# One-core hybrid transformer: float32r head sums, regrouped inverses and an earlier first preparation in the RWKV layer; a third value tile up front in the neighbourhood attention

## The chip, the core and the metric

The kernel runs on one core of a Trainium2 chip. The metric is the device time of one execution in microseconds (us); the kernel before takes 2552.61 us (median of three runs, 2551.04 to 2557.27). The execution that was profiled took 2547.62 us, with a span from its first to its last instruction of 2545.2 us. The engines are named as the profile names them: PE is TensorE (PEld its weight loads), DVE is VectorE, ACT is ScalarE, POOL is GpSimd, and SP is the queue that issues the DMAs.

## The reference, cut to what matters

Four layers work on 256 latent and 256 context tokens of 1024 features, all in float32. The mixers are grouped-query attention (layers 0 and 3), neighbourhood attention (layer 1) and a bidirectional RWKV-7 (layer 2). Each mixer is followed by a normalization, an MLP with squared ReLU, and another normalization. What the change touches is this:

```
# neighbourhood attention (layer 1)
q, k, v = split(h @ wqkv, 3)
# RWKV (layer 2), per token, 16 heads of 64 features
g  = sigmoid(xg @ g1) @ g2
kk = k * k_k ;  kk = kk * rsqrt(max(sum_head(kk*kk), 1e-12))
# ... two scans over the tokens (forwards and backwards) give y ...
mu = mean_head(y) ; var = mean_head((y - mu)**2)
y  = (y - mu) * rsqrt(var + eps) * lnx_g + lnx_b
bonus = sum_head(r * (k_dir0 + k_dir1) * r_k) * v
y  = ((y + bonus) * g) @ wo
```

## The kernel before

**Products.** Activations lie with features on the partitions and the 512 tokens in the free dimension. A float32 product is made of three float32r products: both operands are split into a high part (a cast to float32r on ACT) and a low part (a subtraction on DVE), and high by high, high by low and low by high are summed in one PSUM bank (`mm3`, L430 to L432; `gemm_v`, L479 to L481, for the values, which have tokens on the partitions). The weights come as 363 tiles of 128x1024, in the order of `plan()`; each is loaded by SP (`load_to`), cast by ACT and completed by DVE (L280), a few tiles ahead of their use (`W.depth`). These tiles, the split activations (`pair`, `k4`) and much else share one ring of 36 SBUF tiles of 128x1024.

**Order.** The program text gives each piece of work its place, and the tile framework's scheduler orders each engine's instructions at build time from that, pulling a piece ahead where its inputs and buffers are free by its own model. On the chip every engine then works strictly in its order.

**Neighbourhood attention, opening.** The layer before ends with its latent tokens last, so `opening` runs the context half of the new layer's first products (tokens 256 to 511, tiles 2 and 3) while the latent half is being normalized: after pass `at[0]` it issues `centre`, after pass `at[1]` it issues `finish` (`finish` is one small sum on PE, L537, two ACT steps, and then the scaling and splitting of the eight feature tiles of `h`). The passes are `values(0)` and `values(1)` for the context tokens; `together` (L848 on) then does the same two value tiles for the latent tokens, feature tile by feature tile as `h` arrives. `values(2)` and `values(3)` follow for all tokens.

**RWKV, up to the recurrence.** Six token-shifted mixtures of `h` are made, each of eight 128x512 tiles: a DVE multiply-add (L1025), an ACT cast and a DVE subtraction (L425). After the receptances, `low` makes three low-rank products in turn: `rw_w1` (decay), `rw_a1` and `rw_g1` (output gate, then a Sigmoid into `sig`), each waiting for its own mixture; the mixture of the keys is made after that of the gate. Then come eight `keys(c)`, and the values in eight steps (four weight tiles by two token halves). The rest is a list `todo` (L1561 on) of pieces with a place on a common axis, sorted: `core(c)` covers c to c+1, `prep(c)` c-2.4 to c-.9, `inverses(c)` c-.65 to c-.1, `post(c)` c+1 to c+1.6, keys -2.6 to -1.5, values -1.35 to .3.

**One c of the RWKV** is one 128-feature tile (two heads).
- `prep(c)`: gate products (`wps`) with Sigmoids on ACT, `unit_k` (square on ACT, head sum `kss` by a matmul with the block matrix `ones64`, two logarithm-table steps), decays (scans), products for both directions, `triangles` (`tps`), `solve`: 16x16 triangular systems on POOL, with DMAs through DRAM before and after (`dr`, `lane`, `rr`, `S`).
- `inverses(c)`: the transpose `R` of `S`, then `corner` (`pa`), `both` (`pb`), `spread`, `level1` (`pv`) and `level1b` (`px`), small 32x32 matmuls that join the solved blocks.
- `core(c)`: eight blocks of 64 tokens in both directions. Each block goes `zps` (PE), copy `z` (ACT), `ups` (PE), copy `u` (ACT), `sps` (PE), one or two DVE steps to the next state `s`, and from there to the next block's `zps`; masked products `nps`, transposes `bkt` and outputs `yps` stand between.
- `post(c)`: `mean` (head sum `gm`), `bonus` (head sum `bo`, transposed values `vT`), `var` (head sum `gv`), `normed`, `gated` (product `g` of `g2` and `sig`), `parts`.

The four head sums of a c are plain float32 matmuls of 128x128 by 128x512. PSUM has eight banks: `ps_mm` has three, `ps_s` two, `ps_x` two, `ps_o` one; the sums, `pa`, `pb`, `vT`, `g` and half of `wps` go through `ps_s`.

Of the kernel before, what the change touches and what calls it, by code (L numbers as in the profile page):

```python
# [36 lines left out]
def plan():  # L37

    g = []
    for i in range(DEPTH):  # L40
        if i % 3 == 0:
            a = i // 3
            g += [("att_wqkv", a, "T", 0, n) for n in (8, 9)]
            g += [("att_wqkv", a, "V", kh, 5) for kh in range(2)]
            g += [("att_wqkv", a, "T", 0, n) for n in range(8)]
            g += [("att_wo", a, "T", 0, n) for n in range(8)]
        elif i % 3 == 1:
            g += [("na_wqkv", 0, "V", kh, 8 + j) for j in range(4) for kh in range(2)]
            for c in range(8):
                g += [("na_wqkv", 0, "T", 0, 8 + c), ("na_wqkv", 0, "T", 0, c)]  # L50
            g += [("na_wo", 0, "T", 0, n) for n in range(8)]
        else:
            g += [("rw_wr", 0, "T", 0, n) for n in range(8)]
            g += [("rw_w1", 0, "L", 0, 0), ("rw_a1", 0, "L", 0, 0), ("rw_g1", 0, "T", 0, 0)]
            g += [("rw_wk", 0, "T", 0, n) for n in range(8)]
            g += [("rw_wv", 0, "V", kh, j) for j in range(4) for kh in range(2)]
            g += [("rw_wo", 0, "T", 0, n) for n in range(8)]
        for w, q in MLP_ORDER:
            if w == "1":
                g += [("mlp_w1", i, "T", 0, 8 * q + n) for n in range(8)]  # L60
            else:
                g += [("mlp_w2", i, "T", q, n) for n in range(8)]
    return g
# [130 lines left out]
def dit_kernel(ctx: ExitStack, tc: tile.TileContext, places, t_in, out, layers=DEPTH):  # L194
# [266 lines left out]
        mm3(ps, w, h[KC - 1], 0, 512, KC - 1, False, True)  # L461
        return ps

    def gemm_v(h, parts, toks):

        out = []
        for x, t in enumerate(toks):
            if x % 2 == 0:
                ps_b = bank(ps_mm, 512, "vps")
# [12 lines left out]
        return out  # L482
# [348 lines left out]
    def natten(i, h, gate, nrm, begun, ends):  # L831
        V = [k4("nV") for _ in range(4)]
        kept = {}

        def values(j, toks):
            def part(kh):
                def go():
                    if (j, kh) not in kept:
                        kept[j, kh] = W.next("na_wqkv", 0, "V", kh, 8 + j)
                    return kept[j, kh]  # L840
                return go

            def go():
                for t, ps in zip(toks, gemm_v(h(), [part(0), part(1)], toks)):
                    act.copy(out=V[t][:, j * 256:(j + 1) * 256], in_=ps)
            return go

        def together():  # L848

            ps = [bank(ps_mm, 512, "vps").rearrange("p (t d) -> p t d", t=2) for _ in range(2)]  # L850
            for c in range(KC):
                for j in range(2):
                    vh, vl = (w[:, (c % 4) * 256:(c % 4) * 256 + 256] for w in kept[j, c // 4])
                    for t in range(2):
                        sh, sl = (h()[c][:, y, t * 128:(t + 1) * 128] for y in range(2))
                        pe.matmul(ps[j][:, t], lhsT=sh, rhs=vh, start=c == 0 and t == 0, stop=False)
                        pe.matmul(ps[j][:, t], lhsT=sh, rhs=vl, start=False, stop=False)
                        pe.matmul(ps[j][:, t], lhsT=sl, rhs=vh, start=False, stop=c == 7 and t == 1)
            for j in range(2):
                for t in range(2):  # L860
                    act.copy(out=V[t][:, j * 256:(j + 1) * 256], in_=ps[j][:, t])

        opening(begun, (0, 1), lambda cnd: [values(0, TOKS[1]), values(1, TOKS[1])] if cnd else [together], at=(0, 0))
        kept.clear()
        values(2, range(4))()
        values(3, range(4))()
        kept.clear()
        h = h()
# [93 lines left out]
    def rwkv(i, hx, gate, nrm, begun, ends):  # L962
# [35 lines left out]
        dve.tensor_scalar(out=ka1, in0=C("k_a", "rw"), scalar1=-1.0, scalar2=1.0, op0=ALU.mult, op1=ALU.add)  # L998


        xx = [pair("xx") for _ in range(4)]


# [102 lines left out]
        made[1](PM)  # L1106
        act.activation(out=lora[:, 0], in_=ps, func=AF.Tanh)
        ps = low("rw_a1", "L", made[1])
        made[2](PM)
        act.copy(out=lora[:, 1], in_=ps)  # L1110
        ps = low("rw_g1", "T", made[2])
        made[3](PM)
        act.activation(out=sig, in_=ps, func=AF.Sigmoid)
        m = made[3](KC)
        W.limit = PLAN.index(("rw_wo", 0, "T", 0, 0))
        W.depth = 2

        def keys(c):
            def go():
                if c == 9:  # L1120
                    W.depth = 1
                keep(c, 1, gemm(W.next("rw_wk", 0, "T", 0, c), m, ALL))
                if c == 7:
                    made[4](PM)
            return go
# [36 lines left out]
        def prep(c):  # L1162
# [5 lines left out]
            def gate_products():  # L1168
# [4 lines left out]
                for x, (key, bias) in enumerate((("sg", "w0"), ("ag", "a0"))):  # L1173
                    for d in range(2):
# [7 lines left out]
                            dve.memset(b8(t)[:, :, 0:1], 0.0)  # L1182
                            dst, ps = b8(t)[:, :, 1:65], b8(ps)
                        todo.append(dict(out=dst, in_=ps, bias=C(bias, "rw")[:, d, c:c + 1]))
                sigmoids(todo)
            out.append(gate_products)

            def unit_k():
                sq = tmp(512, "ksq")
                act.activation(out=sq, in_=k_, func=AF.Square, scale=C("k_k", "rw")[:, c:c + 1])  # L1190
                ps = bank(ps_s, 512, "kss")
# [285 lines left out]
        def post(c):  # L1477
            q = st[c]
            hold = {}

            def mean():
                y = tmp(512, "y")
                act.copy(out=y, in_=q["y"])
                ps = bank(ps_s, 512, "gm")
                pe.matmul(ps, lhsT=ones64, rhs=y, start=True, stop=True)
                dve.scalar_tensor_tensor(out=y, in0=ps, scalar=-1.0 / 64, in1=y, op0=ALU.mult, op1=ALU.add)
                sq = tmp(512, "ysq")
                act.activation(out=sq, in_=y, func=AF.Square)
                hold["y"], hold["sq"] = y, sq

            def bonus():
                ps = bank(ps_s, 512, "bo")
                pe.matmul(ps, lhsT=ones64, rhs=q["rkd"], start=True, stop=True)
                bo = q["rkd"]
                act.copy(out=bo, in_=ps)
# [5 lines left out]
                hold["bo"] = bo  # L1501

            def var():
                ps = bank(ps_s, 512, "gv")
# [8 lines left out]
                affine(y, y, C("lnx_g", "rw")[:, c:c + 1], C("lnx_b", "rw")[:, c:c + 1])  # L1513

            def gated():
                ps = bank(ps_s, 512, "g")
                g2 = sml.tile([128, 128], F32, tag="g2", bufs=1, name="g2")
                sp.dma_start(out=g2, in_=t_in["rws"][c, :, 2])
                pe.matmul(ps, lhsT=g2, rhs=sig, start=True, stop=True)
                y = hold["y"]  # L1520
# [42 lines left out]
        for c in range(8):  # L1563
            main = core(c)
            todo += [(c + x / len(main), f) for x, f in enumerate(main)]
            todo += over(inverses(c), c - .65, c - .1)
            todo += over(post(c), c + 1, c + 1.6) if c < 7 else []
            if c >= RHELD:
                todo.append((c - 2.9, lambda c=c: fetch(c)))
        for c in range(8):  # L1570
# [3 lines left out]
            def step(k, c=c, made_=made_):  # L1574
# [224 lines left out]
```

## Time and profile before

| | us |
|---|---|
| median of three runs (lowest, highest) | 2552.61 (2551.04, 2557.27) |
| the profiled execution | 2547.62 |
| its span | 2545.2 |
| PE busy in the span | 2448.7 (96%) |
| DVE busy | 1664.0 (65%) |
| ACT busy | 1188.7 (47%) |
| POOL busy | 209.2 (8%) |

PE's busy time counts a matmul from its start to its modelled end, and matmuls overlap: a 128x512 float32r matmul lasts 0.39 us and the next starts 0.23 us after it. So what a matmul costs PE is read from start to start, and a full PE still hides nothing else. Lines of a timeline give start, duration, engine, line, operation, output<-inputs and count, and in brackets the idle time before with what ended it.

### The profile page before, as it was taken

The numbers are of one execution on the slowest core, as the hardware profiler recorded it, in microseconds if no ns is written. First come the engines' busy times: TensorE is split into PE (matmuls) and PEld (weight loads), VectorE is DVE, ScalarE is ACT, GpSimd is POOL, SyncE is SP. The second block draws the span as 40 slices with busy tenths as digits, with TensorE's granted clock in tenths as the row PEclk, the third lists the DMA queues.
The fourth block names the chain that finished last, engine by engine and source line by source line (L and its number), as shares of the span: only waits on it lengthen the run. The fifth ranks groups of instructions, "written<-read, shape, count | busy, mean of one in ns | idle before, by whom it ended". The sixth has DMA issues, their size and how long they took to land. (4 is left out here: it accounts for less than half of the span.)

```text
span 2545.2 us, 53184 instructions
## 1 busy us (share of the span) xinstructions
PE 2448.7 (96%) x22337; PEld 2085.8 (82%) x22337; DVE 1664.0 (65%) x3087; ACT 1188.7 (47%) x2226; POOL 209.2 (8%) x383
## 2 busy tenths in 40 slices
PE   8999999999999999999889799899999999998998
PEld 5779888889766988888867677778898888998997
DVE  4567777775566777787786565673567663766555
ACT  3555443244566543334555444544362343465644
POOL 0002000002000110000202112211020000121000
PEclk9999999999999999999999999999999999999999
DMA  8432556642211245665132311210336654223553
GB/s 337 166 127 75 182 189 192 207 157 88 69 55 58 88 152 182 207 205 176 60 112 77 80 28 33 41 20 15 143 107 216 206 184 126 93 68 115 175 184 98
DMA packets 158415, 324.11 MB, mean 127 GB/s; under 512 B 77393, under 2 KB 80993, under 8 KB 158177
## 3 DMA queue, kind: packets, MB, share of 16 engines
q1 hardware_dynamic: 158176, 320.73, 39.8%
q8 instruction: 175, 2.87, 0.5%
q14 instruction: 64, 0.52, 0.1%
HBM read 310.71 MB, written 9.97 MB: 126 GB/s over the span
## 5 line engine op out<-in xcount | busy, mean ns | idle before, releaser
L430 PE MATMUL mm<-h,wh 128*128 128x512 f32 (+1 forms) x1472 | 515.5, 351 | 6.1 <-ACT h L180 4.7
L432 PE MATMUL mm<-h,wl 128*128 128x512 f32 (+1 forms) x1472 | 511.6, 348 | 1.1 <-DVE wl L280 1.1
L280 DVE TENSOR_TENSOR wl<-wr,wh 128x1024 fp32r<-128x1024 f32 x363 | 442.7, 1227 | 103.5 <-ACT wh L180 77.9
L431 PE MATMUL mm<-h,wh 128*128 128x512 f32 (+1 forms) x1472 | 510.0, 347 | 0.3 <-DVE h L425 0.2
L180 ACT CAST wh<-wr 128x1024 fp32r<-128x1024 f32 x363 | 373.8, 1049 | 261.7 <-DVE wl L280 89.2
L430 PE MATMUL mm<-f,wh 128*128 128x512 f32 (+1 forms) x1168 | 397.6, 340 | 0.0
L432 PE MATMUL mm<-f,wl 128*128 128x512 f32 (+1 forms) x1168 | 397.6, 340 | 0.0
L431 PE MATMUL mm<-f,wh 128*128 128x512 f32 (+1 forms) x1168 | 397.0, 340 | 0.0
L430 PEld LDWEIGHTS mm<-h,wh 128*128 128x128 f32 x1472 | 279.4, 190 | 50.0 <-issue 8.8
L432 PEld LDWEIGHTS mm<-h,wl 128*128 128x128 f32 x1472 | 279.8, 190 | 37.1 <-issue 3.0
L431 PEld LDWEIGHTS mm<-h,wh 128*128 128x128 f32 x1472 | 279.8, 190 | 34.5 <-issue 2.8
L431 PEld LDWEIGHTS mm<-f,wh 128*128 128x128 f32 x1168 | 221.6, 190 | 24.7
L430 PEld LDWEIGHTS mm<-f,wh 128*128 128x128 f32 x1168 | 221.6, 190 | 24.5
L432 PEld LDWEIGHTS mm<-f,wl 128*128 128x128 f32 x1168 | 221.6, 190 | 24.2
L180 ACT ACTIVATE relu<-mm 128x512 f32<-128x512 f32 (+1 forms) x146 | 72.5, 497 | 360.4 <-PE mm L432 360.3
L425 DVE TENSOR_TENSOR f<-sqr,f 128x512 fp32r<-128x512 f32 (+1 forms) x146 | 82.4, 567 | 210.4 <-ACT f L180 210.4
L492 DVE SCALAR_TENSOR_TENSOR x<-mm,gate,x 128x256 f32<-128x256 f32 x280 | 127.3, 480 | 128.5 <-PE mm L432 128.3
L544 POOL TENSOR_SCALAR x<-zc,cs 128x256 f32<-128x256 f32 x88 | 86.0, 990 | 1302.9 <-DVE zc L575 1302.9
L387 DVE SCALAR_TENSOR_TENSOR mwt<-mwt,srow 128x1024 f32<-128x1024 f32 x144 | 175.8, 1221 | 8.3 <-DMA mwt<-in_mwr_dram 6.9
L387 DVE SCALAR_TENSOR_TENSOR mpr<-mwt,srow 128x1024 f32<-128x1024 f32 x112 | 136.7, 1220 | 0.5
L430 PE MATMUL mm<-o,wh 128*128 128x256 f32 (+1 forms) x400 | 120.1, 302 | 0.3 <-ACT o L180 0.2
L432 PE MATMUL mm<-o,wl 128*128 128x256 f32 (+1 forms) x400 | 119.9, 300 | 0.1
(292 smaller groups left out, 4317.9 us busy)
## 6 DMA issues: line engine op xcount, KB each, us to landing
wr<-in_gw_dram SPq DMA_DIRECT2D x363, 512.0 KB, 3.7
mwt<-in_mwr_dram SPq DMA_DIRECT2D x144, 512.0 KB, 4.3
mwt<-in_mw_dram SPq DMA_DIRECT2D x48, 512.0 KB, 5.4
srow<-srow_d SPq DMA_DIRECT2D x6, 512.0 KB, 4.1
nab<-in_nab_dram SPq DMA_DIRECT2D x8, 384.0 KB, 3.3
rk<-rk_d SPq DMA_DIRECT2D x6, 512.0 KB, 5.1
rk_d<-rkp SPq DMA_DIRECT2D x10, 256.0 KB, 2.2
x<-in_xt_dram SPq DMA_DIRECT2D x4, 512.0 KB, 10.2
```

The lines of the kernel that those rows point to most:

```text
L180: x = f(*args, **kw)
L280: self.lo[self.done % len(self.lo)].tensor_tensor(out=lo, in0=t, in1=hi.bitcast(F32), op=ALU.subtract)
L387: dve.scalar_tensor_tensor(out=to, in0=t, scalar=1.0, in1=rw_["s"][cnd], op0=ALU.mult, op1=ALU.mult, accum_out=m[:, cnd, r * 8 + c:r * 8 + ...
L425: eng.tensor_tensor(out=dst[:, 1, a:b], in0=src, in1=dst[:, 0, a:b].bitcast(F32), op=ALU.subtract)
L430: pe.matmul(ps, lhsT=st, rhs=hl[:, 0, a:b], start=first, stop=False)
L431: pe.matmul(ps, lhsT=st, rhs=hl[:, 1, a:b], start=False, stop=False)
L432: pe.matmul(ps, lhsT=wl[:, c * 128:(c + 1) * 128], rhs=hl[:, 0, a:b], start=False, stop=last)
L492: dve.scalar_tensor_tensor(out=xc(c)[:, a:b], in0=ps[:, a - base:b - base], scalar=gate[:, cnd, c:c + 1], in1=xc(c)[:, a:b], op0=ALU.mult, ...
L544: (eng or dve).tensor_scalar(out=dst, in0=src, scalar1=ca, scalar2=cb, op0=ALU.mult, op1=ALU.add)
```

## The change

In `natten`, the context passes take three value tiles (the second and third in `ps_x` banks) and `finish` is issued after the second pass; `together` does three value tiles for the latent tokens, and only `values(3)` is left for all tokens at once. In `rwkv`, all four head sums split their operand into float32r parts and use two float32r matmuls with a float32r copy of `ones64`; the mean is subtracted by a third matrix (`less64`, identity minus 1/64). `unit_k` is cut in two steps; `post` has eight steps, with the splits as steps of their own, `bo` and `gm` side by side, and the gate's product `g` beside `gv`. `rw_g1` moves behind `rw_wk` tile 3: its mixture is made two tiles per key, its product stands in `keys(3)` with a copy in place of the Sigmoid, which joins the Sigmoids of `prep(1)`. `inverses` is cut in two groups, at c-.74 to c-.42 and c-.28 to c-.06, and `prep(0)` runs from -2.55 to -1.9.

```diff
@@ plan
-            g += [("rw_w1", 0, "L", 0, 0), ("rw_a1", 0, "L", 0, 0), ("rw_g1", 0, "T", 0, 0)]
-            g += [("rw_wk", 0, "T", 0, n) for n in range(8)]
+            g += [("rw_w1", 0, "L", 0, 0), ("rw_a1", 0, "L", 0, 0)]
+            g += [("rw_wk", 0, "T", 0, n) for n in range(4)]
+            g += [("rw_g1", 0, "T", 0, 0)]
+            g += [("rw_wk", 0, "T", 0, n) for n in range(4, 8)]
@@ natten
-            ps = [bank(ps_mm, 512, "vps")... for _ in range(2)]
+            ps = [bank(ps_mm, 512, "vps")... for _ in range(3)]
             for c in range(KC):
-                for j in range(2):
+                for j in range(3):
...
-        opening(begun, (0, 1), lambda cnd: [values(0, TOKS[1]), values(1, TOKS[1])] if cnd else [together], at=(0, 0))
+        opening(begun, (0, 1), lambda cnd: [values(j, TOKS[1], OPEN[j + 2]) for j in range(3)] if cnd else [together], at=(0, 1))
         kept.clear()
-        values(2, range(4))()
         values(3, range(4))()
@@ rwkv
+        sums64 = sml.tile([128, 128], F32R, tag="sums64", bufs=1, name="sums64")
+        act.copy(out=sums64, in_=ones64)
+        less64 = sml.tile([128, 128], F32R, tag="less64", bufs=1, name="less64")
+        dve.scalar_tensor_tensor(out=less64, in0=ones64, scalar=-1.0 / 64, in1=ident, op0=ALU.mult, op1=ALU.add)
+        def in_parts(src):
+            t = pair("ip", F32R)
+            split(t, src, 0, 512)
+            return t
+        def over_heads(ps, w, parts):
+            for x in (1, 0):
+                pe.matmul(ps, lhsT=w, rhs=parts[:, x], start=x == 1, stop=x == 0)
...
         ps = low("rw_a1", "L", made[1])
-        made[2](PM)
+        made[3](PM)
         act.copy(out=lora[:, 1], in_=ps)
-        ps = low("rw_g1", "T", made[2])
-        made[3](PM)
-        act.activation(out=sig, in_=ps, func=AF.Sigmoid)
         m = made[3](KC)
@@ keys
                 keep(c, 1, gemm(W.next("rw_wk", 0, "T", 0, c), m, ALL))
+                if c < 4:
+                    made[2](2 * c + 2)
+                if c == 3:
+                    act.copy(out=sig, in_=low("rw_g1", "T", made[2]))
@@ prep
-                sigmoids(todo)
+                sigmoids(todo + ([dict(out=sig, in_=sig)] if c == 1 else []))
-            def unit_k():
+            def square_k():
                 sq = tmp(512, "ksq")
                 act.activation(out=sq, in_=k_, func=AF.Square, scale=C("k_k", "rw")[:, c:c + 1])
+                q["ksq"] = in_parts(sq)
+            def unit_k():
                 ps = bank(ps_s, 512, "kss")
-                pe.matmul(ps, lhsT=ones64, rhs=sq, start=True, stop=True)
+                over_heads(ps, sums64, q.pop("ksq"))
@@ post
-            def mean():
-                y = tmp(512, "y")
-                act.copy(out=y, in_=q["y"])
-                ps = bank(ps_s, 512, "gm")
-                pe.matmul(ps, lhsT=ones64, rhs=y, start=True, stop=True)
-                dve.scalar_tensor_tensor(out=y, in0=ps, scalar=-1.0 / 64, in1=y, op0=ALU.mult, op1=ALU.add)
-                sq = tmp(512, "ysq")
-                act.activation(out=sq, in_=y, func=AF.Square)
+            def taken():
+                hold["yp"], hold["bp"] = in_parts(q["y"]), in_parts(q["rkd"])
+            def centred():
+                po, ps = bank(ps_s, 512, "bo"), bank(ps_s, 512, "gm")
+                over_heads(po, sums64, hold.pop("bp"))
+                over_heads(ps, less64, hold.pop("yp"))
+                y, sq = tmp(512, "y"), tmp(512, "ysq")
+                act.activation(out=sq, in_=ps, func=AF.Square)
+                act.copy(out=y, in_=ps)
+                act.copy(out=q["rkd"], in_=po)
+            def squares():
+                hold["sp"] = in_parts(hold["sq"])
@@ post: bonus keeps vT and now also issues the load of g2; var:
-                pe.matmul(ps, lhsT=ones64, rhs=hold["sq"], start=True, stop=True)
+                ps, hold["g"] = bank(ps_s, 512, "gv"), bank(ps_s, 512, "g")
+                over_heads(ps, sums64, hold.pop("sp"))
+                pe.matmul(hold["g"], lhsT=hold["g2"], rhs=sig, start=True, stop=True)
...
-            return [mean, bonus, var, normed, gated, parts]
+            return [taken, centred, squares, bonus, var, normed, gated, parts]
@@ todo
-            todo += over(inverses(c), c - .65, c - .1)
+            inv = inverses(c)
+            todo += over(inv[:6], c - .74, c - .42) + over(inv[6:], c - .28, c - .06)
...
-            todo += over([step(k) for k in range(9)], c - 2.4, c - 1.5)
-            todo += over([step(k) for k in range(9, 13)], c - 1.4, c - .9)
+            todo += over([step(k) for k in range(10)], *((c - 2.4, c - 1.5) if c else (-2.55, -1.9)))
+            todo += over([step(k) for k in range(10, 14)], c - 1.4, c - .9)
```

## Rows read from the trace of the kernel before

**Rows 1.** The page's first part: busy time of each engine.
```profile
PE 2448.7 (96%) x22337; PEld 2085.8 (82%) x22337; DVE 1664.0 (65%) x3087; ACT 1188.7 (47%) x2226; POOL 209.2 (8%) x383
```
**Rows 2.** Busy time by stretch: bounds and length, engines (count), PE clock, DMA share, GB/s.
```profile
1293.00:1332.00 39.00, 32.31 (x107) 20.48 (x106) 36.19 (x55) 23.96 (x38) 2.31 (x3) 0.91 0.24 75
1332.00:1377.00 45.00, 45.00 (x244) 34.35 (x243) 26.90 (x42) 20.97 (x31) 0.44 (x2) 1.00 0.36 109
...
1655.00:1702.00 47.00, 43.47 (x1208) 35.00 (x1209) 29.39 (x63) 23.75 (x53) 10.44 (x32) 0.96 0.15 21
...
1776.00:1811.00 35.00, 34.03 (x754) 28.13 (x754) 15.67 (x31) 13.22 (x32) 0.00 (x0) 1.00 0.48 184
```
**Rows 3.** Timeline (start, us, engine, line, operation): PE, float32r matmuls in a stream.
```profile
1195.37 0.39 PE L430 MATMUL mm<-f,wh 128*128 128x512 f32 x1
1195.60 0.39 PE L431 MATMUL mm<-f,wh 128*128 128x512 f32 x1
```
**Rows 4.** Timeline of PE: head sums of the first tile, and what follows them.
```profile
1512.95 1.12 PE L1485 MATMUL gm<-y,cs_rw 128*128 128x512 f32 x2
1513.91 1.02 PE L1493 MATMUL bo<-ag,cs_rw 128*128 128x512 f32 x2
1514.87 0.45 PE L1440 MATMUL sps<-u,bkt 64*64 64x64 f32 x8
...
1517.16 1.13 PE L1505 MATMUL gv<-ysq,cs_rw 128*128 128x512 f32 x2
1518.21 0.45 PE L1426 MATMUL ups<-z,Xt 64*64 64x64 f32 x8
```
**Rows 5.** Waits of PE, 1455 to 1811 us: total, times, longest.
```profile
PE kss L1192 <- ACT ksq L180: 6.9, 5, 1.5
...
PE pv L1357 <- DVE xd L1344: 2.4, 5, 1.2
```
**Rows 6.** Groups by line, 1455 to 1811 us: busy, mean ns, idle before.
```profile
L425 DVE TENSOR_TENSOR o<-y,o 128x512 fp32r<-128x512 f32 x7 | 4.8, 692 | 0.9
...
L180 ACT CAST o<-y 128x512 fp32r<-128x512 f32 x7 | 4.3, 618 | 9.8 <-DVE y L1522 9.8
```
**Rows 7.** Timeline, one block of the recurrence in tile 1.
```profile
1531.92 0.45 PE L1414 MATMUL zps<-rV,nmo 64*64 64x64 f32 x8
...
1533.61 0.27 ACT L180 COPY u<-ups 128x128 f32<-128x128 f32 x1 [0.64 <-PE ups L1426]
...
1537.52 0.40 PE L1440 MATMUL sps<-u,bkt 64*64 64x64 f32 x8
...
1538.30 0.29 DVE L1447 TENSOR_TENSOR s<-s,fcol 128x128 f32<-128x128 f32 x1
```
**Rows 8.** Timeline of PE, opening of the neighbourhood attention.
```profile
600.51 0.28 PE L481 MATMUL vps<-wh,h 128*128 128x256 f32 x1
601.10 0.70 PE L537 MATMUL pvar<-s,cs 128*128 128x256 f32 x2 [0.31 <-DVE s L530]
604.96 0.39 PE L856 MATMUL vps<-wh,h 128*128 128x256 f32 x1 [3.16 <-ACT h L180]
```
**Rows 9.** Busy time of the stretch right after, columns as in rows 2.
```profile
605.00:610.00 5.00, 5.00 (x28) 4.84 (x29) 3.24 (x8) 5.00 (x13) 5.00 (x7) 0.66 0.00 2
```
**Rows 10.** Timeline of DVE: mixtures of the keys.
```profile
1318.99 2.08 DVE L1025 SCALAR_TENSOR_TENSOR mix<-xx,cs_rw,x 128x512 f32<-128x512 f32 x3
...
1326.58 2.08 DVE L1025 SCALAR_TENSOR_TENSOR mix<-xx,cs_rw,x 128x512 f32<-128x512 f32 x3
```
**Rows 11.** Waits of PE, 1293 to 1455 us: total, times, longest.
```profile
PE pa L1322 <- DVE R L1313: 3.9, 1, 3.9
PE vps L479 <- ACT wh L180: 3.5, 1, 3.5
```
**Rows 12.** Timeline of SP around the first tile's solution.
```profile
1402.04 0.38 SPq L1297 DMA_DIRECT2D S<-rr  x1
1402.46 1.54 SPq L270 DMA_DIRECT2D wr<-in_gw_dram  x2
```

More of the change, by code (lines that the diff above doesn't have):

```diff
@@ L462, in end, with gemm_v @@
         return ps
-    def gemm_v(h, parts, toks):
+    def gemm_v(h, parts, toks, pool=None):
         out = []
@@ L468, in gemm_v @@
             if x % 2 == 0:
-                ps_b = bank(ps_mm, 512, "vps")
+                ps_b = bank(pool or ps_mm, 512, "vps")
             out.append(ps_b[:, (x % 2) * 256:(x % 2) * 256 + 256])
@@ L833, in natten, with values @@
         kept = {}
-        def values(j, toks):
+        def values(j, toks, pool=None):
             def part(kh):
@@ L843, in go @@
             def go():
-                for t, ps in zip(toks, gemm_v(h(), [part(0), part(1)], toks)):
+                for t, ps in zip(toks, gemm_v(h(), [part(0), part(1)], toks, pool)):
                     act.copy(out=V[t][:, j * 256:(j + 1) * 256], in_=ps)
@@ L848, in together @@
         def together():
-            ps = [bank(ps_mm, 512, "vps").rearrange("p (t d) -> p t d", t=2) for _ in range(2)]
+            ps = [bank(ps_mm, 512, "vps").rearrange("p (t d) -> p t d", t=2) for _ in range(3)]
             for c in range(KC):
-                for j in range(2):
+                for j in range(3):
                     vh, vl = (w[:, (c % 4) * 256:(c % 4) * 256 + 256] for w in kept[j, c // 4])
@@ L858, in together @@
                         pe.matmul(ps[j][:, t], lhsT=sl, rhs=vh, start=False, stop=c == 7 and t == 1)
-            for j in range(2):
+            for j in range(3):
                 for t in range(2):
                     act.copy(out=V[t][:, j * 256:(j + 1) * 256], in_=ps[j][:, t])
-        opening(begun, (0, 1), lambda cnd: [values(0, TOKS[1]), values(1, TOKS[1])] if cnd else [together], at=(0, 0))
+        opening(begun, (0, 1), lambda cnd: [values(j, TOKS[1], OPEN[j + 2]) for j in range(3)] if cnd else [together], at=(0, 1))
         kept.clear()
-        values(2, range(4))()
         values(3, range(4))()
@@ L1184, in gate_products @@
                         todo.append(dict(out=dst, in_=ps, bias=C(bias, "rw")[:, d, c:c + 1]))
-                sigmoids(todo)
+                sigmoids(todo + ([dict(out=sig, in_=sig)] if c == 1 else []))
             out.append(gate_products)
-            def unit_k():
+            def square_k():
                 sq = tmp(512, "ksq")
                 act.activation(out=sq, in_=k_, func=AF.Square, scale=C("k_k", "rw")[:, c:c + 1])
+                q["ksq"] = in_parts(sq)
+            out.append(square_k)
+            def unit_k():
                 ps = bank(ps_s, 512, "kss")
-                pe.matmul(ps, lhsT=ones64, rhs=sq, start=True, stop=True)
+                over_heads(ps, sums64, q.pop("ksq"))
+                sq = tmp(512, "ksr")
                 dve.tensor_scalar(out=sq, in0=ps, scalar1=1e-12, scalar2=None, op0=ALU.max)
@@ L1479, in post @@
             hold = {}
-            def mean():
-                y = tmp(512, "y")
-                act.copy(out=y, in_=q["y"])
-                ps = bank(ps_s, 512, "gm")
-                pe.matmul(ps, lhsT=ones64, rhs=y, start=True, stop=True)
-                dve.scalar_tensor_tensor(out=y, in0=ps, scalar=-1.0 / 64, in1=y, op0=ALU.mult, op1=ALU.add)
-                sq = tmp(512, "ysq")
-                act.activation(out=sq, in_=y, func=AF.Square)
+            def taken():
[8 more added lines that the diff above has]
+                act.copy(out=q["rkd"], in_=po)
                 hold["y"], hold["sq"] = y, sq
+            def squares():
+                hold["sp"] = in_parts(hold["sq"])
             def bonus():
-                ps = bank(ps_s, 512, "bo")
-                pe.matmul(ps, lhsT=ones64, rhs=q["rkd"], start=True, stop=True)
                 bo = q["rkd"]
-                act.copy(out=bo, in_=ps)
                 pt = bank(ps_s, 512, "vT")
@@ L1501, in bonus @@
                 hold["bo"] = bo
+                hold["g2"] = sml.tile([128, 128], F32, tag="g2", bufs=1, name="g2")
+                sp.dma_start(out=hold["g2"], in_=t_in["rws"][c, :, 2])
             def var():
-                ps = bank(ps_s, 512, "gv")
-                pe.matmul(ps, lhsT=ones64, rhs=hold["sq"], start=True, stop=True)
+                ps, hold["g"] = bank(ps_s, 512, "gv"), bank(ps_s, 512, "g")
+                over_heads(ps, sums64, hold.pop("sp"))
+                pe.matmul(hold["g"], lhsT=hold["g2"], rhs=sig, start=True, stop=True)
                 r = hold["sq"]
@@ L1515, in gated @@
             def gated():
[L1516 to L1520, printed above, removed]
+                y, ps = hold["y"], hold["g"]
                 dve.tensor_tensor(out=y, in0=y, in1=hold["bo"], op=ALU.add)
```

2 lines of the change are left out of this document (removed).

## The prediction

> **What bounds the kernel now.** I read the page's busy times first: PE is busy 96% of the span, DVE 65%, ACT 47% [rows 1]. So time is won where PE's own work becomes less or where PE stands. The busy time by stretch shows where it stands: nowhere in the keys (45.00 of 45 us), for 6.7 of 39 us in the low-rank products, for about 3.5 us of 47 in a middle tile of the RWKV recurrence and 1.0 of 35 in a late one [rows 2]. The waits of PE then name the releasers [rows 5, 11], and timelines give the price of one matmul from start to start, since durations overlap [rows 3, 4]. The change touches only the opening of the neighbourhood attention and the RWKV layer, so all other stages keep their time.
>
> **Part 1, head sums in float32r.** A plain float32 sum of 128x512 holds PE for 0.96 us beside another such sum (gm to bo, bo to sps) and 1.05 us alone between small products (gv to ups) [rows 4]. A float32r matmul of that size holds it for 0.23 us (1195.37 to 1195.60) [rows 3]; a new sum is two, 0.46 us, plus the 0.09 us by which the lone sum is dearer than the paired one. Per tile: kss 1.05 to 0.55; gm and bo 1.92 to 0.92 plus 0.09; gv 1.05 to 0.46, since g now follows it directly and pays the switch. That is 4.02 to 2.02, so 2.0 us, times eight tiles 16 us. PE is the engine that sets the pace there [rows 2], so I count all 16; bounds 5 (each new matmul at its full duration of 0.39 and every sum with the switch) and 17 (no switch).
>
> The Trainium skill (TensorE: Matmul & The Clock Gate, section Back-to-back issue gap) gives about 131 ns per matmul of 512 columns in a sustained stream. By it the 64 new matmuls would cost 8.4 us where the row's 0.23 gives 14.7, and the sums would save 22 us; the trace's stream is at 0.23, so I keep to the row.
>
> What it adds: four splits per tile, each an ACT cast (0.62) and a DVE subtraction (0.69) [rows 6], less one DVE operation of the same size: 2.5 us of ACT and 2.1 of DVE per tile. In a middle tile DVE works 29.4 of 47 us and ACT 23.8 [rows 2]; with a tile of 43 us they come to 31.5 and 26.3, so the cover is PE's other work. The extra operations stand in order before the copies of z and u and the state's update. One block of the recurrence takes 1531.92 to 1533.88 and 1537.52 to 1538.59, 3.0 us, and u then waited 3.6 us for PE to come to sps [rows 7]: a copy that is 0.6 us late is mostly hidden. I charge 4 us in all for those that are not, bounds 0 and 12.
>
> **Part 2, steps spread in the recurrence.** PE waits 6.9 us for the square of kk in five tiles [rows 5], because square and sum are one step. Now square and split stand a step (a tenth of a tile, over 4 us) before the sum. Two more operations (1.3 us) come into the chain but fit in that. I count 5; bounds 0 and 6.9. The pause between the two groups of the inverses is for the wait of pv on the transpose xd, 2.4 us [rows 5]: I count 1, bounds -2 (a solution that comes late) and 2.4. The last tile's `post` has two splits more, but two products of the output weights stand beside it: 0, bounds -1 and 2.
>
> **Part 3, neighbourhood opening.** PE ends the second context pass at 600.51+0.12, does the small sum and starts again at 604.96: 4.3 us less 0.4 for the sum, 3.9 us of standing [rows 8]. Then 28 matmuls of 256 columns take 5.00 us at a granted clock of 0.66, a mix of 2.4 and 1.2 GHz after the idle stretch [rows 9]; at the 0.12 us of the full rate they are 3.4 us, so 1.6 us more. The third pass is 48 matmuls, 5.8 us, all of it work that is only moved, and it covers the 3.5 us between the small sum and the first `h` tile. The latent tiles then meet 18 matmuls (2.2 us) each instead of 12. What is queued: two more weight tiles are split before `together`, after the steps of `finish` in the text's order, and their loads stand earlier on SP. Twelve weight parts, where eight were, lie in the ring of 36, so the tiles for `values(3)` may come late; they have 17 us. I count 5.4, bounds 2 and 6.
>
> **Part 4, output gate beside the keys.** DVE is busy 36.2 of 39 us in the low-rank stretch, PE 32.3 [rows 2]: the mixtures set the pace. A group of three takes 3.8 us (1318.99 to 1326.58 is two) [rows 10], so the eight tiles of the gate's mixture, 10.1 us, no longer stand before the keys' own. PE's 24 matmuls of the gate, 5.4 us, move behind `keys(3)`, where PE is full, and are paid there: net 4.7 us. The cover for the mixture is the keys' stretch, DVE 26.9 of 45 us [rows 2]; it becomes 37 of 50. Without that cover the 10.1 us come back. The added demand is tiles: 16 mixture tiles at once instead of about 11. I count 5, bounds -4 and 7. The weight tile `rw_g1` moves on SP, ACT and DVE behind four key tiles, at the same cost. The Sigmoid of `sig` moves into `prep(1)`: 0.6 us before the gates of tile 1, at a time when values run: 0.
>
> **Part 5, first preparation sooner.** PE stands 3.9 us for R, the transposed first solution, and then 3.5 us for a weight tile [rows 11]. That tile's load stands on SP directly behind the read-back of the same solution [rows 12], so one cause sets both. `triangles` of tile 0 move from behind keys 5 and 6 to about keys 3 and 4, `solve` from behind key 7 to before key 5; two keys are 48 matmuls, 10.9 us, ahead of the values, against 7.4 needed. Thirteen small DMAs (eight dr, two lane, two rr, one S) and POOL's work move with it, past the key tiles' loads; none is a new one. I count 5.5, bounds 0 and 7.4. Late next are the values' own mixture and the copies into V; nothing here shortens them.
>
> **Sum.** 16 - 4 + 5 + 1 + 5.4 + 5 + 5.5 = 34 us (33.9). Against the profiled execution, 2547.6 - 34 = 2513.6. The median of the runs lies 5.0 us above that execution, so the forecast is 2518.6.
>
> **Rivals.**
> - *All waits go.* The cover holds everywhere and no new wait comes: 17 + 6.9 + 2.4 + 6 + 7 + 7.4 = 46.7 us, 2506. For it: every term has its releaser in a row. Against it: the scheduler plans by its own times, and a reordered stretch gets waits of its own.
> - *Waits only move.* The sums (16 - 4) and the opening (5.4) pay; the RWKV stages before the recurrence find DVE or the ring of tiles late and give back their 10.5, and the kss wait goes to another operation: 17 us, 2535. For it: DVE is busy 93% of the low-rank stretch.
> - *Given back by the tile ring.* Keys 2 to 4 wait for weights that find no free tile, some 6 us each (load, cast, subtraction), and the gate's mixture delays the first preparation: 18 us on top of the case before: about 2553, no change.
> - *Slower: the two `ps_s` banks.* `g` now holds one of two banks from `var` to `gated`, 0.17 of a tile, 8 us, at the place of pa and pb of the next tile. If PE, which works in order, stands through that in seven tiles, it loses 56 us against 34 of gain: 2575. It decides from 4.9 us per tile on. Against it: pa and pb are four short groups, each freed by one DVE step.
> - *The queues in order.* ACT and DVE get 4.6 us more per tile. If all of it lands on the recurrence, that is 37 us for eight tiles in place of the 4 charged: 2552. Rows 7 show 3.6 us to spare in a block of 6.5, and a late tile of 35 us has 4.4 per block against 3.0, so I take it as unlikely, and put it with the no-change case.
>
> The Trainium skill (PSUM — Partial Sum Buffer, section Engine vs sequencer instructions) states that ACT's and DVE's queues are strictly first in, first out. By it a split whose input is late holds back the copy of z behind it, which is the last rival; the trace has no such split yet, so it shows neither.
>
> **How the numbers follow.** The forecast 0.57, all waits go 0.13, waits only move 0.18, no change (ring or queues) 0.06, slower 0.06. A measurement of this kernel can tell about 0.3%, 8 us, from no change, so faster means under 2545. Faster 0.88, same 0.06, slower 0.06. The range takes the forecast's own terms with their bounds and most of the two neighbours: 2502 to 2540.
>
> **What would show it.** Right: kss, gm, bo and gv as pairs 0.23 us apart; no wait of kss on ksq; PE without the stretch of 4 us near 601, and its clock at 2.4 GHz after it; keys(0) ending about 10 us sooner after the second low-rank product; R before PE comes to pa; middle tiles of 43 us instead of 47. Wrong: waits of PE on `ip`, or on a `ps_s` bank around g; keys that wait for wh or wl; a recurrence whose tiles keep their 47 us though PE has less to do.

## The result and the profile after

The changed kernel takes 2521.86 us (median of four runs, 2519.41 to 2523.17) beside 2551.82 us for the kernel before on the same chip: a ratio of 0.9882, 95% interval 0.9864 to 0.9899, or 30 us less (26 to 35). Forecast were 34 us less and 2518.6. The profiled execution took 2522.02 us with a span of 2520.2, 25.0 less than before's, whose profiled execution was 4 us below its median. One of the four executions of e9 (below) took 3552 us at a granted clock of 0.618 and is left out of its ratio.

The total hides errors that cancel. The marks below are read from the timelines of PE (first `low`, first `zps`, last `yps` of a tile) and ACT (start of the last cast into `o` of tile 7), us:

| stage | before | after | forecast of the difference |
|---|---|---|---|
| start to the first attention score of layer 1 | 654.3 | 650.0 | -5.4 |
| from there to the first `low` | 639.4 | 639.4 | 0 |
| first `low` to first `zps` | 161.6 | 151.2 | -10.5 |
| first `zps` to `o` of tile 7 | 364.3 | 353.8 | -18 |
| a middle tile (mean of tiles 1 to 4) | 47.4 | 45.0 | -4 |
| the rest | 725.6 | 725.8 | 0 |

The recurrence (first `zps` to `o`) gained 10.5 us where parts 1 and 2 add up to 18.

The page's first part, after, answers to [rows 1]: DVE has 11.5 us more and ACT 18.3 (the splits), PE 13.2 less.

```profile
PE 2435.5 (97%) x22337; PEld 2088.5 (83%) x22337; DVE 1675.5 (66%) x3112; ACT 1207.0 (48%) x2260; POOL 210.1 (8%) x383
```

Busy time by stretch, after, with the columns of [rows 2]: the low-rank products, the keys and a middle tile. In the low-rank stretch, ten us shorter, PE and DVE now work equally long. The keys take 52 us in place of 45. In the middle tile PE stands 4.1 of 45 us, before some 3.5 of 47: its work became less, its standing did not. The keys' longer stretch holds the gate's 24 matmuls and two new waits, of kss and of tps (lines below).

```profile
1289.00:1318.00 29.00, 26.17 (x84) 16.28 (x83) 26.45 (x44) 17.78 (x27) 2.37 (x3) 0.88 0.15 48
1318.00:1370.00 52.00, 49.29 (x261) 38.45 (x261) 36.89 (x53) 28.16 (x40) 8.41 (x24) 1.00 0.40 116
...
1627.00:1672.00 45.00, 40.89 (x1226) 34.38 (x1222) 31.70 (x67) 26.72 (x58) 11.27 (x34) 1.00 0.20 36
```

Timeline of PE, after, two head sums of the first tile, answering to [rows 4]. A pair of matmuls holds PE for 0.57 us (bo to gm) and 0.55 (gm to sps); kss and gv, between small products, 0.66. Over all 32 sums the starts add up to 18.9 us, before to 32.3: 13.4 saved where the prediction had 16.

```profile
1495.88 0.74 PE L1014 MATMUL bo<-ip,sums 128*128 128x512 f32 x2
1496.45 0.62 PE L1014 MATMUL gm<-ip,less 128*128 128x512 f32 x2
1497.00 0.45 PE L1457 MATMUL sps<-rV,bkt 64*64 64x64 f32 x8
...
1504.63 0.73 PE L1014 MATMUL gv<-ip,sums 128*128 128x512 f32 x2
1505.29 0.44 PE L1424 MATMUL bkt<-cs,BK 64*64 64x64 f32 x6
```

Waits of PE, after, in the recurrence (total, times, longest), answering to [rows 5]. kss on ksq (6.9) and pv on xd (2.4) are gone; yps now waits for `ip`, the split that holds the bank of the outputs before, and zps for the state more than before (0.9).

```profile
PE ups L1446 <- ACT z L182: 4.1, 11, 0.6
PE yps L1477 <- DVE ip L427: 3.6, 5, 0.7
PE zps L1438 <- DVE s L1467: 3.4, 6, 0.6
```

Timeline of PE, after, in the neighbourhood opening, answering to [rows 8]: the third context pass runs on both sides of the small sum, with nothing waited for.

```profile
602.47 0.28 PE L481 MATMUL vps<-wh,h 128*128 128x256 f32 x1
602.59 0.59 PE L539 MATMUL pvar<-s,cs 128*128 128x256 f32 x2
602.83 0.47 PE L482 MATMUL vps<-wl,h 128*128 128x256 f32 x1
```

The stretch of [rows 9], after: the clock is granted in full (2.4 GHz) in place of 0.66; PE was busy for all of the 4 us ahead of it.

```profile
605.00:610.00 5.00, 5.00 (x44) 5.00 (x44) 4.62 (x9) 5.00 (x14) 5.00 (x4) 1.00 0.03 11
```

Waits of PE, after, from the low-rank products to the first `nps`, answering to [rows 11]: pa still waits 2.4 for R (3.9 before). The wait for the weight tile (3.5) is 0.2 now; that for the values' mixture `mh` stays, 2.4 before (first line) and 3.0 after. The waits of tps and kss, in the keys, are new.

```profile
PE vps L479 <- ACT mh L180: 2.4, 1, 2.4
```

```profile
PE vps L481 <- ACT mh L182: 3.0, 1, 3.0
...
PE pa L1342 <- DVE R L1333: 2.4, 1, 2.4
...
PE tps L1283 <- DVE BK L1240: 1.4, 1, 1.4
PE kss L1014 <- DVE ip L427: 1.3, 1, 1.3
...
PE vps L481 <- ACT wh L182: 0.2, 1, 0.2
```

### The profile page after: what moved, and what is told of

It reads as the page before. It is cut to its first block, busy times and chain, and to the rows that moved or that the text cites. A ratio compares the mean times of both kernels' runs of the same rounds, so it can differ in the third digit from the quotient of the medians.

```text
span 2520.2 us, 53253 instructions
## 1 busy us (share of the span) xinstructions
PE 2435.5 (97%) x22337; PEld 2088.5 (83%) x22337; DVE 1675.5 (66%) x3112; ACT 1207.0 (48%) x2260; POOL 210.1 (8%) x383
## 4 chain that ended last, share of the span: by engine, by line
PE 88%; ACT 5%; DVE 4%; issue 1%; DMA 1%; POOL 0%; SPq 0%; ACTq 0%; DVEq 0%; POOLq 0%
PE mm L432 22%; PE mm L434 21%; PE mm L433 21%; PE ptp L654 2%; PE op L803 1%; PE op L922 1%; PE mdp L324 1%; PE vps L481 1%; PE vps L483 1%; PE vps L482 1%; PE bkt L1424 1%; PE ups L1446 1%; PE nps L1414 1%; PE sc L891 1%; PE tps L1283 1%
```

## The experiments

Ratios are to the kernel before on the same chip (medians 2547.97, 2549.56 and 2548.67 for the groups e1 to e4, e5 to e8, e9 to e12). Differences "to after" are of ratios, times 2550 us.

**First, the parts.** e1 is the kernel before with the diff's natten part alone.

> Kernel before with only the third value tile in the neighbourhood opening. Theory (the opening's standing PE and its slow clock are the whole gain there): 5.5 us less than the kernel before, the first scores of layer 1 begin 5 to 6 us sooner, every later stage keeps its length. Rival (the gain is given back by late weight tiles, since 12 parts lie in the ring of 36): under 2 us less, with PE waiting for wh or wl in values(3) or the first keys.

Measured: 2540.33 us, 0.9969 (0.9959 to 0.9979), 8 us less than before (5 to 10). The theory holds: the first score of layer 1 starts at 649.0 us instead of 654.3. The other stages of its profile differ from before's by up to 3.2 us, though their code is the same, so stage times of one profile are no surer than that.

e2 is the kernel before with the float32r sums and the new steps of `prep` and `post`, but the old inverses:

```diff
-            inv = inverses(c)
-            todo += over(inv[:6], c - .74, c - .42) + over(inv[6:], c - .28, c - .06)
+            todo += over(inverses(c), c - .65, c - .1)
```

> Kernel before with only the float32r head sums and the new steps of post and unit_k; opening, gate, first preparation and inverses as before. Theory (sums give 16 us of PE and 7 of the kss wait, and the splits' own waits give back about 12): 10 to 14 us less than the kernel before, all between the first zps and the last. Rival A (the splits cost next to nothing, the other parts took the gain): 20 us less. Rival B (nothing comes of the sums, the inverses' place gives the gain): under 4 us less.

Measured: 2562.11 us, 1.0055 (1.0039 to 1.0072): 14 us slower than before. Tiles 1 to 4 take 51.4 us on average. The sums by themselves lose, though PE has less to do. The theory missed; rival B has the right place, the inverses, but no expectation had a loss.

e3 puts the output gate back (mixture, product and weight tile between `rw_a1` and the keys):

```diff
-            g += [("rw_w1", 0, "L", 0, 0), ("rw_a1", 0, "L", 0, 0)]
-            g += [("rw_wk", 0, "T", 0, n) for n in range(4)]
-            g += [("rw_g1", 0, "T", 0, 0)]
-            g += [("rw_wk", 0, "T", 0, n) for n in range(4, 8)]
+            g += [("rw_w1", 0, "L", 0, 0), ("rw_a1", 0, "L", 0, 0), ("rw_g1", 0, "T", 0, 0)]
+            g += [("rw_wk", 0, "T", 0, n) for n in range(8)]
@@ and low("rw_g1") with its Sigmoid ahead of the keys
```

> Changed kernel with the output gate back among the low-rank products. Theory (the gate's move gave 2 to 3 us before the recurrence, not the 5 forecast, since 5.4 us of its matmuls came back among the keys and new waits of kss and tps with them): 1 to 4 us more than the changed kernel. Rival (the move is worth the forecast 5 or more, and something else in the keys took 4 us): 5 to 8 us more.

Measured: 2518.2 us, 0.9885 (0.9867 to 0.9903): as after, and less than either expectation. The 5 us of the gate are not there.

e4 puts the first preparation back:

```diff
-            todo += over([step(k) for k in range(10)], *((c - 2.4, c - 1.5) if c else (-2.55, -1.9)))
+            todo += over([step(k) for k in range(10)], c - 2.4, c - 1.5)
```

> Changed kernel with prep(0) back at -2.4 to -1.5. Theory (the earlier first solution removed the waits for R and for the weight tile queued behind it on SP): 5 to 8 us more than the changed kernel, PE waiting again over 3 us for pa or for wh near the first inverse. Rival (keys that end sooner or the gate's move already made the solution early enough): within 2 us of the changed kernel.

Measured: 2514.38 us, 0.987 (0.9852 to 0.9888), the lowest time of all kernels. The theory missed: PE does wait for R again (lines below), but the 5.5 us of the earlier preparation are not there either.

**The loss of e2.** In e2 the copies of `spread` (`Xt<-M`, four per tile) stood on ACT right behind two table loads and four Sigmoids. e5 to e7 test whether that is it: e5 is after with the edit of e2 (the old inverses), e7 is before with the new inverses alone, e6 is after with float32 sums in the new places:

```diff
-            for x in (1, 0):
-                pe.matmul(ps, lhsT=w, rhs=parts[:, x], start=x == 1, stop=x == 0)
+            pe.matmul(ps, lhsT=w, rhs=parts, start=True, stop=True)
@@ no split; sums64, less64 in F32; y copied once by ACT
```

> The kernel after with only the inverses put back into one group at c-.65 to c-.1; all else as after. Theory (the regrouping is what lets the sums pay, because it takes the copies of spread out of ACT's stretch of table load, four Sigmoids and table load): middle tiles of about 51 us as in e2 instead of 45, so 25 to 35 us slower than after (2545 to 2557), zps and ups of PE waiting for the v and z copies of ACT, and a granted clock of 0.90 to 0.95 in the middle tiles. Rival (the prediction's price, 1 us): within 5 us of after, 2520 to 2527. Second rival (the jam in e2 came from the gate's or the preparation's old place): middle tiles stay at 45 to 46 us.

Measured: 2552.91 us, 1.0017 (1.0007 to 1.0027), 34 us over after. As the theory said: all of the change's gain hangs on two lines priced at 1 us. Waits of PE in e5's recurrence: no kss wait either, with square and sum in separate steps; but waits for ACT's copies z and v.

```profile
PE ups L1446 <- ACT z L182: 11.9, 14, 1.6
PE zps L1434 <- ACT v L182: 9.9, 6, 2.0
```

> The kernel after with the four head sums as plain float32 matmuls (sums64 and less64 in float32, one matmul for each sum, no split; y is copied once by ACT), with every step in its new place. Theory (the float32r pairs save PE's time, 2.0 us a tile by the prediction, 16 us in all, against 4.6 us of splits on ACT and DVE per tile that cost part of it): 3 to 16 us slower than after, 2524 to 2538; gm, bo and gv 0.96 to 1.05 us each. Rival (what pays is the new place of the steps and of the inverses, and the splits cost as much as the pairs save): within 3 us of after or faster, 2512 to 2524.

Measured: 2528.22 us, 0.9918 (0.9906 to 0.993), 9 us over after. Its 32 sums add up to 32.2 us on PE, 13.3 more than after's, but first `zps` to `o` of tile 7 is only 7.5 us longer (361.2 against 353.8). The theory holds, and by this difference the splits and what they delay cost about 6 us of the 13.

> The kernel before with only the two groups of the inverses (c-.74 to c-.42 and c-.28 to c-.06). Theory (the regrouping takes the copies of spread out of ACT's stretch between two table loads, and without the splits there is little behind them): 2 to 8 us faster than before, middle tiles of 46 to 47 us, the wait of pv on xd gone. If the regrouping were worth as much without the sums as with them, 25 us or more faster. Rival (prediction, 1 us): within 3 us of before.

Measured: 2541.75 us, 0.997 (0.9958 to 0.9982), 8 us less than before; tiles 1 to 4 take 45.2 us on average. Its waits of PE in the recurrence no longer list kss or z among the large ones, with square and sum still one step; the regrouping alone brings them from 6.9 (kss) and 5.2 us (z) to 0.4 and 1.1:

```profile
PE ups L1426 <- ACT z L180: 1.1, 1, 1.1
```

Sums alone +14, regrouping alone -8, but both together about -19 (e8 below at -27, less the opening's -8): 25 us that belong to neither alone.

**Which half of the regrouping?** e9 keeps the new place of the first six steps, the last of which is `spread`; e10 that of the last four:

```diff
@@ e9
-... + over(inv[6:], c - .28, c - .06)
+... + over(inv[6:], c - .283, c - .1)
@@ e10
-over(inv[:6], c - .74, c - .42) + ...
+over(inv[:6], c - .65, c - .344) + ...
```

> The kernel after with the first six steps of the inverses in their new place (c-.74 to c-.42, spread the last of them) and the last four in the old one (c-.283 to c-.1). Theory (ACT's queue: what pays is that spread's copies of 2.5 us stand before the table loads and the four Sigmoids): within 6 us of after, 2516 to 2528, middle tiles of 45 to 46 us. Rival (the gap before pv, or the later end of the solution, is what pays): 20 us or more slower than after, middle tiles of 49 to 51 us.

Measured: 2519.52 us, 0.9884 (0.9866 to 0.9902): as after, as the theory said. Mean of tiles 1 to 4: 45.9 us.

> The kernel after with the first six steps of the inverses in their old place (c-.65 to c-.344) and the last four in the new one (c-.28 to c-.06). In ACT's order spread's copies then stand behind the second table load, as in e5, and the copies of v and z behind them in the order of after. Theory: 20 to 32 us slower than after, 2540 to 2554, middle tiles of 49 to 51 us and a granted clock under 0.95 there. Rival (the gap pays): within 6 us of after.

Measured: 2548.84 us, 0.9996 (0.9987 to 1.0004), 29 us over after, again as the theory said; mean of tiles 1 to 4: 50.2 us. So what pays is the earlier place of the first six steps. That place also makes the pause before `pv`: 0.14 of a tile in after, 0.137 in e9, 0.064 in e10; so the two runs by themselves don't part the pause from ACT's order. PE's waits do: pv waits 2.9 us for xd in e10, which is what the pause is for, and 8.9 us for ACT's copy v, which after doesn't wait for.

```profile
PE pv L1377 <- ACT v L182: 8.9, 6, 1.8
...
PE pv L1377 <- DVE xd L1364: 2.9, 5, 0.8
```

Of the six steps `spread` alone has work on ACT, and in the middle tiles its four copies stand right behind the second table load in before, e2, e5 and e10, and ahead of the first in after, e7 and e9: the kernels with middle tiles of 47 to 51 us and those of 45 to 46 part just there. No run moves `spread` alone. The timeline of ACT in e10, tile 4, shows how (start, us, then in brackets the idle time before and its end). Table load, four Sigmoids, table load, four Xt copies and the square fill 1680.07 to 1689.4, but for 1.00 us; v comes at 1689.35, z at 1690.02.

```profile
1680.07 1.28 ACT L182 ACT_TABLE_LOAD   x1
1681.37 1.27 ACT L182 ACTIVATE sg<-wps,cs_rw 128x512 f32<-128x512 f32 x2
1683.63 1.27 ACT L182 ACTIVATE ag<-wps,cs_rw 128x512 f32<-128x512 f32 x2 [1.00 <-PE wps L1192]
1684.90 1.28 ACT L182 ACT_TABLE_LOAD   x1
1686.20 2.50 ACT L182 COPY Xt<-M 32x512 f32<-32x512 f32 x4
1688.72 0.72 ACT L182 ACTIVATE ksq<-rk,cs_rw 128x512 f32<-128x512 f32 x1
1689.35 0.25 ACT L182 COPY v<-pv 128x128 f32<-128x128 f32 x1
...
1690.02 0.27 ACT L182 COPY z<-zps 128x128 f32<-128x128 f32 x1
```

The same stretch of after: the Xt copies begin nine us ahead of the first load, in gaps where ACT had nothing to do (2.29 us idle before the first), and z follows the first table load by 6.3 us instead of 9.95.

```profile
1650.51 1.25 ACT L182 COPY Xt<-M 32x512 f32<-32x512 f32 x2 [2.29 <-DVE M L1358]
...
1652.07 1.24 ACT L182 COPY Xt<-M 32x512 f32<-32x512 f32 x2
...
1659.32 1.28 ACT L182 ACT_TABLE_LOAD   x1
1660.62 1.26 ACT L182 ACTIVATE sg<-wps,cs_rw 128x512 f32<-128x512 f32 x2
1661.77 1.26 ACT L182 ACTIVATE ag<-wps,cs_rw 128x512 f32<-128x512 f32 x2
1663.06 1.28 ACT L182 ACT_TABLE_LOAD   x1
...
1665.64 0.27 ACT L182 COPY z<-zps 128x128 f32<-128x128 f32 x1
```

And PE's clock pays a second time. Busy time of e10 in stretches of 5 us (columns as in [rows 2]): PE works 3.15 of 5 us while ACT is behind, the granted clock falls to 0.77 and then to 0.55, near the level of 1.2 GHz. PE is then busy 5.00 of 5 us with 94 matmuls; at the full clock behind it 110 need 3.69.

```profile
1687.00:1692.00 5.00, 3.15 (x69) 2.68 (x70) 0.90 (x2) 3.94 (x10) 1.13 (x5) 0.77 0.24 30
1692.00:1697.00 5.00, 5.00 (x94) 4.16 (x94) 2.50 (x6) 2.15 (x5) 0.00 (x0) 0.55 0.34 56
1697.00:1702.00 5.00, 3.69 (x110) 3.34 (x112) 3.66 (x7) 4.14 (x10) 0.00 (x0) 1.00 0.01 5
```

In after the same place (1661 to 1671) is at 1.00 throughout: PE works 4.28 and 4.81 of 5 us.

```profile
1661.00:1666.00 5.00, 4.28 (x148) 3.62 (x148) 3.53 (x8) 4.97 (x10) 4.32 (x9) 1.00 0.02 3
1666.00:1671.00 5.00, 4.81 (x142) 3.97 (x130) 3.05 (x7) 2.86 (x8) 0.78 (x2) 1.00 0.24 31
```

**Gate and first preparation.** e8 is after with both in their old places (the edits of e3 and e4).

> The kernel after with both the output gate and the first preparation in their old places; opening, sums, new steps and regrouped inverses as in after. Theory (e3 and e4 add: each of the two moves costs 2 to 6 us): 6 to 10 us faster than after, 2512 to 2516, keys that end as late as before but low, keys and values together no longer than in e4. Rival (they are two ways of paying the same wait, so that without either the wait for R and for the first values' weights, 7.4 us, comes back): equal to after or up to 8 us slower.

Measured: 2523.7 us, 0.9896 (0.9882 to 0.991). The rival holds for the time, and half for its reason: the wait for R is back, that for the values' weights is not.

```profile
PE pa L1339 <- DVE R L1330: 5.1, 1, 5.1
...
PE vps L479 <- ACT wh L180: 0.3, 1, 0.3
```

From first `low` to first `zps` the four kernels make a square:

| | preparation old | preparation sooner |
|---|---|---|
| gate old | 155.66 (e8) | 152.46 (e3) |
| gate beside the keys | 149.12 (e4) | 151.23 (after) |

The gate alone saves 6.5 us, the preparation alone 3.2, both 4.4. Repeats of this stage's code agree within 0.5 us in two cases (149.1 and 148.7 in e4 and e12, 151.2 and 151.4 in after and e9) and differ by 1.7 in a third (161.6 and 163.3 in before and e1). So the gate's 6.5 is clear of that, and so is that the two don't add up to 9.7; whether the preparation costs 2 us beside the gate stays open. In whole times all this is too small to be told apart from the runs.

Why the two don't add: DVE works through its order. In after, SP issues the load of S at 1377.64 (first fence) and it lands 3.3 us later; R follows at 1396.23 (second fence), since it stands behind copies of the values and steps of `prep(1)`, which wait for PE and ACT.

```profile
1377.64 0.39 SPq L1317 DMA_DIRECT2D S<-rr  x1
```

```profile
1394.40 0.57 DVE L1157 COPY rV<-vps 64x128 f32<-64x128 f32 x2
1395.01 1.31 DVE L1226 TENSOR_TENSOR cc<-sg 128x520 f32<-128x520 f32 x2
1396.23 0.70 DVE L1333 STREAM_TRANSPOSE R<-S 128x512 f32<-128x512 f32 x1
```

In e4 the load is issued at 1387.35, ten us later, and R stands at 1390.95, right after it lands; PE waits 5.6 us for it, but the keys (from the end of `keys(0)` to the last one's last matmul) are 4.0 us shorter than in after (48.2 against 52.2) and the values' mixture is waited for less:

```profile
PE pa L1342 <- DVE R L1333: 5.6, 1, 5.6
...
PE vps L481 <- ACT mh L182: 2.3, 1, 2.3
```

e11 puts the preparation between the two places.

```diff
-*((c - 2.4, c - 1.5) if c else (-2.55, -1.9))
+c - 2.4, c - (1.5 if c else 1.75)
```

> The kernel after with the first preparation between its two places: ten steps at -2.4 to -1.75 (before -2.4 to -1.5, after -2.55 to -1.9); the gate beside the keys. Theory (the early place pushes DVE and ACT work into the keys that the gate's mixture already fills, the late one leaves PE 5.6 us for R): R comes some 3 us sooner than in e4, keys as long as in e4: 0 to 4 us faster than e4, 2510 to 2515. Rival (any move forward costs the keys what it saves at pa): 2514 to 2520.

Measured: 2520.72 us, 0.9889 (0.9875 to 0.9902), 152.5 us for the stage: a miss for the theory, and 0.7 us beyond the rival's range. The keys are short (47.8), R is waited for as in after, but the wait for the weight tile is back:

```profile
PE vps L481 <- ACT wh L182: 4.5, 3, 3.6
...
PE pa L1342 <- DVE R L1333: 2.4, 1, 2.4
```

e12 is e4 with y copied out of PSUM before its split, to shorten the hold of the bank that yps waits for:

```diff
-                hold["yp"], hold["bp"] = in_parts(q["y"]), in_parts(q["rkd"])
+                y = tmp(512, "y0")
+                act.copy(out=y, in_=q["y"])
+                hold["yp"], hold["bp"] = in_parts(y), in_parts(q["rkd"])
```

> e4 (the kernel after with the first preparation in its old place) and y copied by ACT from PSUM to SBUF before its split, so that its PSUM bank is free one DVE step sooner. Theory: the wait of yps on ip (3.6 us in five tiles) goes, against 0.6 us more of ACT per tile: 0 to 3 us faster than e4, 2511 to 2514.5. Rival (the copy only delays ACT's queue, and a bank freed sooner is not what ends the wait): 1 to 5 us slower than e4, 2515 to 2519.

Measured: 2521.86 us, 0.9899 (0.9885 to 0.9912), 7 us over e4, as the rival said or a little more. The intervals just overlap, but in the profiles the recurrence takes 358.3 us against 350.9. The wait for ip (3.6) became one of 2.4 for y, and ups waits 8.0 us for z where it was 4.5: 0.6 us more per tile on ACT come out as more than they save.

```profile
PE ups L1446 <- ACT z L182: 8.0, 15, 1.2
...
PE yps L1477 <- ACT y L182: 2.4, 5, 0.5
```

## Why the prediction came out right, and where its steps failed

- **Part 1 (16 saved, 4 given back).** Right in kind. The pairs save 13.4 us, not 16: each holds PE for 0.55 to 0.66 us against the 0.46 to 0.55 reckoned. About 6 us are given back (e6), so 7.5 net where 12 were forecast. (The lower bound of 5 is 4.3 if all four sums pay the switch, as it says.) The upper bound of 12 for what is given back was wrong: with the old inverses the recurrence (first `zps` to `o` of tile 7) is 381.6 us in e5, 28 longer than in after, with the same sums. The Trainium skill (TensorE: Matmul & The Clock Gate, Back-to-back issue gap) would have had 131 ns per matmul and 22 us; the traces bear out the dearer reading, 0.28 us and more.
- **Part 2 (5 for kss, 1 for the regrouping).** The step that failed. The kss wait does go, but either edit removes it, the new steps (e5) or the regrouping (e7); and the regrouping is worth 8 us alone and 29 to 34 with the sums (e10, e5). It was read as a gap for pv on xd, 2.4 us; with the six steps back in their old place (e10) that wait is 2.9 us of the 29 lost. What the prediction left out is where ACT's Xt copies stood: behind two table loads.
- **The rival "queues in order".** It had a share in the 0.06 for no change, and its size, 37 us, is near what e2 (a recurrence 17.5 us longer than before's, though the sums take PE 12 us less) and e5 show. It named the right kind of mechanism, ACT's order ahead of z, though the place of `spread` decides it and not the splits alone, and this change comes with its remedy. The slack of rows 7 was that of one block in mid-tile, and the jam lies at the block where the Sigmoids stand. The Trainium skill (PSUM — Partial Sum Buffer, Engine vs sequencer instructions) has ACT's and DVE's queues strictly first in, first out; z behind Xt in e10, and R behind `cc` in after, fifteen us past the landing of S, agree.
- **Part 3 (5.4).** Right: the 3.2 us of standing and the low clock are gone. The stage is 4.2 us shorter in after and 5.3 in e1, whose whole time is 8 us (5 to 10) less.
- **Parts 4 and 5 (5 and 5.5).** As a sum too high: against e8 the two moves give 4.4 for 10.5. Both were priced from the kernel before, each as if alone. `keys(0)` ends 9.2 us sooner, about as forecast, but the keys take 8.4 us longer: the gate's 24 matmuls, 5.9 us, and the new waits of tps and kss, 2.7 us. That R would be there before PE was wrong: the solution is in SBUF, but DVE's order holds R. That one cause sets the wait for R and that for the weight tile was wrong too: with the late preparation e8 waits 5.1 and 0.3 us for them, with a sooner one e11 2.4 and 4.5. What sets the second is not shown.
- **What made up for it.** The first inverses, too, gain from the regrouping: first `low` to first `zps` is 4.9 us longer in e5 than in after, which no term had. So that stage came out as forecast, 10.4 us shorter, but less than half of it by the two moves. The recurrence did not (10.5 us of 18): the pairs bring 7.5 net, and new steps and regrouping together 3.0 of 6 (e6 against before). That 34 forecast and 30 measured agree better than their terms is luck.
- **The rivals on banks.** No wait on a `ps_s` bank around g shows among after's waits, and no key waits for a free tile; "all waits go" failed on the longer or new waits of zps, nps and yps. Of the signs of being wrong, a wait on `ip` (yps, 3.6 us) came, and the middle tiles stopped at 45.0 us instead of 43.
- **Open.** Tiles 5 and 6 take 41.6 and 35.7 us in after, 39.4 and 34.7 before; e12 shows no gain from freeing the outputs' bank, and the cause was not tested further. e4 is 7.5 us below after in time, but 3 us by the ratios, whose intervals overlap: it is no slower than after, and that it is faster isn't settled.

## What to carry to other kernels

An edit that only moves work is priced on each engine's order, not at the wait that it is meant for: list what stands around it on ACT and DVE, and what is queued behind. Where two edits draw on the same cover (ACT's stretch between table loads; DVE during the keys), price them together and try them alone and together: here +14 and -8 made -19, and 6.5 and 3.2 made 4.4. A stall that leaves PE idle for some us costs again through the granted clock behind it.

## What was not expected of the hardware

- One late engine cost the recurrence twice: behind the stretch in e10 in which PE was busy for 3.15 of 5 us, the granted clock was 0.55, near 1.2 GHz, and a kss pair took 1.15 us in e5's middle tiles (0.66 in after).
- A switch of ACT's table costs the load and no more in these traces: the load starts at 1659.32, 0.02 us after the copy before it ends, and the Sigmoids at 1660.62, 1.30 us later. The Trainium skill (ScalarE: Activation LUTs, What ACT_TABLE_LOAD costs) gives 1283 ns and a drain of 1380 ns; the trace shows the first and not the second, and none of after's 17 loads starts more than 0.02 us behind the instruction before it.
